# Moving the on-chip arenas of a hybrid encoder kernel to other addresses

## The chip, the cores and the metric

The kernel runs on one core of a Trainium2 chip. Its engines are TensorE (PE, with its weight loads shown apart as PEld), VectorE (DVE), ScalarE (ACT), GpSimd (POOL) and SyncE (SP), which here issues the DMAs. Operands live in the on-chip memory, 128 partitions wide; TensorE writes its products to eight banks of PSUM. The metric is the time of one execution on the device in microseconds; the kernel before has a median of 2407.32 us over two runs.

## The reference

One layer of a bidirectional encoder is applied to two sequences, a prompt of 512 tokens and a sample of 1024 tokens, of width 1024, all in float32:

```
h    = rms_norm(x, n_pre_mix)
proj = h @ w_in                                  # 1024 x 6688
y_a  = gated_delta(conv(q, k, v), g, beta) both ways, normed, gated @ w_br_gdn
y_b  = hgrn2(q, f, i) both ways, normed, gated @ w_br_hg
x    = x + rms_norm((gate0 * y_a + gate1 * y_b) @ w_out, n_post_mix)
h2   = rms_norm(x, n_pre_ffn)
ff   = (silu(h2 @ w_gate) * (h2 @ w_up)) @ w_down    # 1024 -> 2816 -> 1024
y    = x + rms_norm(ff, n_post_ffn)
```

The gated delta rule and HGRN2 are computed in chunks with small matrix products; the large dense products are those with `w_in`, the two branch weights, `w_out`, `w_gate`, `w_up` and `w_down`.

## The kernel before

**Split products.** A dense product in float32 is made from three products of a rounded type (float32r): each operand x is split into a rounded part `hi` and the rest `lo = x - hi`, and `mm3` adds `hi*hi`, `hi*lo` and `lo*hi` in one bank. The function `split` does this with one ACT copy and one DVE subtraction, which write the two parts into an arena of type float32r. The stationary operand of such a matmul is 128 x 128, the moving one 128 x 512, and every matmul loads its own weights. Where the tokens allow it, the products are arranged in the seven-product scheme of Strassen and Winograd (`seven`, `p2_both`, `down`). The small products of the chunked recurrences are plain float32.

**Stages.** Projections and the two recurrences of both sequences run interleaved until about 1184 us; then come the branch and output products, the gate and up products of the feed-forward part (`alone`, `seven`), and `down` at the end.

**Order.** The kernel writes its own order. `Tape` collects all operations with a cost for each, `schedule` places tiles in slots of pools and sorts the operations by a simulated clock, and `emit` issues them in that order. This is finished before any address is known: only then are the arenas opened and a slot turned into an address by `home`. All engine instructions are recorded at one line, L632, so that rows of the profile are told apart by arena.

**Arenas.** An arena is one on-chip tensor with the slots of a pool side by side. They stand in this order, each starting where the one before it ends:

- from the left: `sa` (constants and small vectors), `ba` (16 slots of 516 words, raw weights and intermediates), `ra` (128 columns of ones, split type), `ha` (4 slots of 4096 words, the split activations h and, later, a ring of split weights), `wa` (6 slots of 1024 words, split weights);
- from the right: `sm` (small tiles), `la` (36 slots of 516 words).

Later `la` and `sm` are closed and `xr` (20 slots of 1024 words, split operands of the feed-forward part) takes their place from the right; `wa` is closed and `xa` opens at its start; at the end `ha` is closed and `da` opens at its start. The constant `SKEW` adds words to `xr`. A slot of `ba`, `la`, `xa` or `da` is 516 words, that is 2064 bytes, so that each next slot starts 16 bytes further modulo 512. The slots and slices of the split arenas are all multiples of 512 bytes, so that within one of them every operand of a matmul starts at the same address modulo 512: 288 in all of them before the change.

In the rows of the profile a matmul is written bank<-moving,stationary; one name stands for both where both lie in the same arena.

Of the kernel before, what the change touches and what calls it, by code (L numbers as in the profile page):

```python
# [12 lines left out]
F32 = mybir.dt.float32  # L13
F32R = mybir.dt.float32r
# [26 lines left out]
HOLD = ((3, 2, 1, 2), (2, 2, 2, 2))  # L41
MSTEP = (24, 28)
PAIR = False
SKEW = 48
URGENT = 100
PO = False
NVEC = 88
# [700 lines left out]
def layer(ctx, tc, x_p, x_s, w_out, n_post_mix, n_post_ffn, w_down, vec, xt_p, xt_s, w_in, w_br, w_gate, w_up,  # L748
# [74 lines left out]
    hpool, wpool = Pool("h", 4, KD * TB), Pool("w", NW, 1024)  # L823
# [1630 lines left out]
    def arena(stack, name, cols, dtype, **kw):  # L2454
        return stack.enter_context(tc.tile_pool(name=name, bufs=1, **kw)).tile([P, cols], dtype, name=name + "_a")

    col = {}
    ends = [0, 0]
    for p in small.values():
        if p.kind == "SB":  # L2460
            b = p in brief
            col[p] = ends[b]
            ends[b] += p.count * p.width
    sa = arena(ctx, "sa", ends[0], F32)
    ba = arena(ctx, "ba", 16 * big.width, F32)
    hs, rs = ExitStack(), ExitStack()
    ra = arena(ctx, "ra", P, F32R)
    ha = arena(hs, "ha", 4 * hpool.width, F32R)
    w1 = ExitStack()
    wa = arena(w1, "wa", NW * 1024, F32R)  # L2470
    sm = arena(rs, "sm", ends[1], F32, side="right")
# [8 lines left out]
    def home(v):  # L2480
# [3 lines left out]
        if p is big or p is xpool:  # L2484
            s = [s for s in p.segs if s.low <= v.at][-1]
            if s.name not in opened:
                if s.name == "xr":
                    rs.close()
                else:
                    w1.close()  # L2490
                    if s.name == "da":
                        hs.close()
                opened[s.name] = arena(w1 if s.name == "xa" else ctx, s.name, s.count * p.width + (SKEW if p is xpool else 0),
                                       F32R if p is xpool else F32, side="right" if p is xpool else "left")
# [69 lines left out]
```

## Time and profile before

| | |
|---|---|
| two runs | 2408.84 and 2405.81 us, median 2407.32 us |
| profiled execution | span 2403.8 us from first to last instruction; no other time of it is listed |
| outside the span | 2407.32 - 2403.8 = 3.5 us, taken from the median |
| TensorE clock granted, mean | 0.999 |
| instructions | 37624, of which 14046 matmuls and as many weight loads |
| busy | PE 99%, PEld 83%, DVE 73%, ACT 52%, POOL 32% of the span |
| DMA | 338.62 MB, mean 141 GB/s |

The page gives for a group of instructions its busy time, the mean duration of one and the idle time before them. A matmul's recorded duration is longer than its place in the stream, since matmuls overlap; what one costs is the distance from its start to the next one's start. That distance is had from the timeline, which gives the start of a run of equal instructions and their number.

### The profile page before, as it was taken

The page shows a single profiled execution, that of the slowest core. Times are in us where ns is not written, and L with a number is a line of the kernel's source. Part 1 is how long each engine was busy: PE and PEld are TensorE (multiplying, and loading weights), DVE is VectorE, ACT ScalarE, POOL GpSimd, SP SyncE. Part 2 cuts the span into 40 slices and gives each one's busy share as a digit, 9 for nine tenths or more (in the row PEclk, how much of TensorE's full clock was granted, in tenths as well). Part 3 has the DMA queues.
Part 4 walks back from the last instruction along what each step waited for, and adds up shares of the span by engine and source line. Part 5 has one row for each costly group of instructions (what it writes and reads, how often), then busy time and mean ns, then how long its engine had stood idle before and what let it go on. Part 6 is the DMA issues. An engine that isn't in the chain of part 4 may idle for free.

```text
span 2403.8 us, 37624 instructions
## 1 busy us (share of the span) xinstructions
PE 2384.2 (99%) x14046; PEld 1991.2 (83%) x14046; DVE 1747.9 (73%) x2820; ACT 1256.1 (52%) x2096; POOL 766.7 (32%) x1021
## 2 busy tenths in 40 slices
PE   8999999999999999999999999999999999999998
PEld 6888888888888888888888888888888888888887
DVE  7878798958859667758767894665887878545566
ACT  6756867646647546647433464444353534433343
POOL 0544426051602513412120001213677675200221
PEclk9999999999999999999999999999999999999999
DMA  5124633411231230332875263543454554674453
GB/s 211 60 78 152 210 102 112 135 55 53 89 84 50 79 97 31 98 97 88 289 287 186 103 225 109 189 152 101 158 178 171 186 183 154 209 251 140 151 204 125
DMA packets 193334, 338.62 MB, mean 141 GB/s; under 512 B 53104, under 2 KB 92528, under 8 KB 193152
## 3 DMA queue, kind: packets, MB, share of 16 engines
q1 hardware_dynamic: 193152, 336.23, 41.8%
q8 instruction: 110, 1.80, 0.3%
q14 instruction: 72, 0.59, 0.1%
HBM read 255.50 MB, written 80.66 MB: 140 GB/s over the span
## 4 chain that ended last, share of the span: by engine, by line
PE 91%; DVE 6%; ACT 1%; issue 1%; DMA 1%; SPq 0%; POOL 0%; DVEq 0%; POOLq 0%
PE bank L632 91%; DVE la_a L632 3%; DVE ba_a L632 2%; DVE wa_a L632 1%; ACT la_a L632 1%; ACT ba_a L632 0%; DVE sm_a L632 0%; DMA la_a<-dram_cr_sc 0%; SPq L632 0%; ACT wa_a L632 0%; DMA ba_a<-lay_w_in 0%; DMA la_a<-dram_w_sc 0%; DMA dram_u_sc<-la_a 0%; DVE da_a L632 0%; ACT ha_a L632 0%
## 5 line engine op out<-in xcount | busy, mean ns | idle before, releaser
L632 PE MATMUL bank<-ha_a,wa_a 128*128 128x512 f32 x5496 | 1321.5, 395 | 1.1 <-DVE wa_a L632 0.9
L632 PEld LDWEIGHTS bank<-ha_a,wa_a 128*128 128x128 f32 x5496 | 1018.4, 188 | 207.5 <-issue 3.3
L632 PE MATMUL bank<-xr_a 128*128 128x512 f32 x1386 | 314.3, 389 | 0.0
L632 PEld LDWEIGHTS bank<-xr_a 128*128 128x128 f32 x1386 | 260.3, 188 | 53.8
L632 PE MATMUL bank<-xr_a,ha_a 128*128 128x512 f32 x1200 | 275.3, 389 | 0.0
L632 PEld LDWEIGHTS bank<-xr_a,ha_a 128*128 128x128 f32 x1200 | 225.4, 188 | 46.6
L632 POOL TENSOR_TENSOR ba_a<-ba_a 128x512 f32<-128x512 f32 (+1 forms) x129 | 168.8, 1314 | 216.5 <-DVE ba_a L632 85.6
L632 ACT ACTIVATE la_a<-la_a 128x512 f32<-128x512 f32 (+1 forms) x300 | 192.7, 658 | 62.9 <-DVE la_a L632 44.5
L632 DVE TENSOR_TENSOR wa_a<-la_a,wa_a 128x1024 fp32r<-128x1024 f32 (+1 forms) x136 | 161.3, 1198 | 58.2 <-PE bank L632 46.7
L632 ACT ACTIVATE wa_a<-la_a 128x1024 fp32r<-128x1024 f32 (+1 forms) x136 | 133.2, 992 | 102.3 <-PE bank L632 96.5
L632 POOL TENSOR_TENSOR la_a<-la_a 128x256 f32<-128x256 f32 (+2 forms) x50 | 60.1, 1210 | 352.7 <-DVE la_a L632 265.7
L632 DVE TENSOR_TENSOR wa_a<-ba_a,wa_a 128x1024 fp32r<-128x1024 f32 (+1 forms) x102 | 115.4, 1147 | 70.4 <-PE bank L632 51.0
L632 ACT ACTIVATE wa_a<-ba_a 128x1024 fp32r<-128x1024 f32 (+1 forms) x102 | 92.9, 928 | 105.5 <-PE bank L632 91.6
L632 ACT ACTIVATE ha_a<-ba_a 128x512 fp32r<-128x512 f32 (+1 forms) x124 | 79.3, 645 | 130.0 <-PE bank L632 110.4
L632 DVE TENSOR_TENSOR ha_a<-ba_a,ha_a 128x512 fp32r<-128x512 f32 (+1 forms) x124 | 129.6, 1053 | 17.7 <-ACT ha_a L632 17.2
L632 POOL TENSOR_TENSOR la_a<-la_a,sm_a 128x30 f32<-128x30 f32 (+43 forms) x248 | 133.2, 537 | 18.2
L632 POOL TENSOR_TENSOR sm_a<-la_a 128x60 f32<-128x60 f32 (+39 forms) x155 | 76.7, 495 | 166.9 <-DMA la_a<-dram_u_sc 156.2
L632 ACT ACTIVATE ba_a<-ba_a 128x512 f32<-128x512 f32 (+1 forms) x181 | 112.7, 633 | 18.9 <-DVE ba_a L632 16.7
L632 DVE TENSOR_TENSOR la_a<-la_a 128x512 f32<-128x512 f32 (+2 forms) x170 | 116.5, 700 | 8.4 <-ACT la_a L632 7.6
L632 PE MATMUL bank<-wa_a,ha_a 128*128 128x512 f32 x528 | 120.1, 390 | 0.0
L632 DVE TENSOR_TENSOR xr_a<-da_a,xr_a 128x1024 fp32r<-128x1024 f32 (+2 forms) x60 | 71.1, 1199 | 64.1 <-ACT xr_a L632 48.1
L632 PEld LDWEIGHTS bank<-wa_a,ha_a 128*128 128x128 f32 x528 | 99.1, 188 | 20.5
(192 smaller groups left out, 3358.1 us busy)
## 6 DMA issues: line engine op xcount, KB each, us to landing
la_a<-lay_w_in SPq DMA_DIRECT2D x79, 512.0 KB, 5.8
ba_a<-lay_w_gate SPq DMA_DIRECT2D x36, 512.0 KB, 4.2
ba_a<-lay_w_up SPq DMA_DIRECT2D x33, 512.0 KB, 3.7
dram_a_sc<-xa_a SPq DMA_DIRECT2D x56, 256.0 KB, 2.1
ba_a<-lay_w_in SPq DMA_DIRECT2D x27, 512.0 KB, 5.5
ba_a<-w_ffn_down SPq DMA_DIRECT2D x24, 512.0 KB, 4.5
da_a<-dram_a_sc SPq DMA_DIRECT2D x22, 512.0 KB, 6.0
ba_a<-dram_a_sc SPq DMA_DIRECT2D x20, 512.0 KB, 5.2
```

Of the source, the lines that this page charges most:

```text
L632: f(*[m(a) for a in o.args], **{k: m(a) for k, a in o.kw.items()})
```

## The change

Three constants and two widths change. `sa` becomes 56 words (224 bytes) longer, so that everything to its right on the left side moves by 224 bytes; `ha` becomes 32 words (128 bytes) longer, so that `wa` moves by another 128; `xr` gets 8 words (32 bytes) more at its end, so that its start, counted from the right, moves down by 32. The added words are never used.

```diff
-SKEW = 48
+SKEW = 56
+LEAD, GAP = 56, 32
...
-    sa = arena(ctx, "sa", ends[0], F32)
+    sa = arena(ctx, "sa", ends[0] + LEAD, F32)
     ba = arena(ctx, "ba", 16 * big.width, F32)
     hs, rs = ExitStack(), ExitStack()
     ra = arena(ctx, "ra", P, F32R)
-    ha = arena(hs, "ha", 4 * hpool.width, F32R)
+    ha = arena(hs, "ha", 4 * hpool.width + GAP, F32R)
```

Starts modulo 512 bytes, before and after:

| arena | before | after |
|---|---|---|
| sa, sm, la | 128, 320, 256 | the same |
| ba | 32 | 256 |
| ra, ha, and da later | 288 | 0 |
| wa, and xa later | 288 | 128 |
| xr | 288 | 256 |

No instruction, wait or DMA is added, removed or moved in the order.

## The prediction

> **What bounds the kernel now.** I read the page first (engines, chain of waits), then the list of what TensorE waited for, then the chain in order of time.
>
> ```profile
> span 2403.8 us, 37624 instructions
> ...
> PE 2384.2 (99%) x14046; PEld 1991.2 (83%) x14046; DVE 1747.9 (73%) x2820; ACT 1256.1 (52%) x2096; POOL 766.7 (32%) x1021
> ...
> PE 91%; DVE 6%; ACT 1%; issue 1%; DMA 1%; SPq 0%; POOL 0%; DVEq 0%; POOLq 0%
> ```
> ```profile
> PE bank L632 <- ACT ba_a L632: 7.1, 1, 7.1
> PE bank L632 <- DVE la_a L632: 1.9, 3, 0.9
> PE bank L632 <- DVE wa_a L632: 1.1, 2, 0.9
> ```
> ```profile
> 1183.59 1212.79 PE bank L632 x5398
> ```
>
> TensorE is busy 99% of the span. It waited 7.1 us once, at the start, and 1.9 and 1.1 us in the next two groups of waits; the rest are smaller. From 1183.59 us to 1183.59 + 1212.79 = 2396.4 us the chain is TensorE alone, without a break. So the time is the sum of the distances between matmul starts, and an address matters if it changes that distance; nothing else has a place to show.
>
> **What a matmul costs now.** The groups of matmuls, shapes kept apart, give the number of each pairing of arenas (moving, stationary):
>
> ```profile
> L632 PE MATMUL bank<-ha_a,wa_a 128*128 128x512 f32 x5496 | 1321.5, 395 | 1.1 <-DVE wa_a L632 0.9 <-ACT wa_a L632 0.2
> ...
> L632 PE MATMUL bank<-xr_a 128*128 128x512 f32 x1386 | 314.3, 389 | 0.0
> L632 PE MATMUL bank<-xr_a,ha_a 128*128 128x512 f32 x1200 | 275.3, 389 | 0.0
> ...
> L632 PE MATMUL bank<-wa_a,ha_a 128*128 128x512 f32 x528 | 120.1, 390 | 0.0
> L632 PE MATMUL bank<-ha_a 128*128 128x512 f32 x480 | 112.1, 389 | 0.0
> ...
> L632 PE MATMUL bank<-wa_a,ra_a 128*128 128x512 f32 x72 | 27.9, 410 | 0.8 <-ACT wa_a L632 0.4 <-DVE wa_a L632 0.3
> ...
> L632 PE MATMUL bank<-xr_a,wa_a 128*128 128x512 f32 x120 | 27.5, 390 | 0.0
> ```
>
> That is 9282 split matmuls. The timeline of TensorE gives their distance, from the start of one run of equal matmuls to the start of the next:
>
> ```profile
> 1416.64 43.68 PE L632 MATMUL bank<-ha_a,wa_a 128*128 128x512 f32 x192
> ```
> ```profile
> 1663.16 13.76 PE L632 MATMUL bank<-xr_a,wa_a 128*128 128x512 f32 x60
> 1676.76 5.60 PE L632 MATMUL bank<-ha_a,wa_a 128*128 128x512 f32 x24
> 1682.20 13.76 PE L632 MATMUL bank<-xr_a,wa_a 128*128 128x512 f32 x60
> ...
> 1701.24 13.76 PE L632 MATMUL bank<-xr_a,ha_a 128*128 128x512 f32 x60
> 1714.84 5.38 PE L632 MATMUL bank<-ha_a 128*128 128x512 f32 x23
> ```
> ```profile
> 2082.04 314.32 PE L632 MATMUL bank<-xr_a 128*128 128x512 f32 x1386
> ```
>
> 60 matmuls from 1663.16 to 1676.76 are 13.60 / 60 = 226.7 ns each; the 24 of the next run (1676.76 to 1682.20) 226.7; the 60 with `ha` as weights (1701.24 to 1714.84) 226.7; the 1386 of `down`, less the 0.39 us tail of the last, (314.32 - 0.39) / 1385 = 226.7; the 192 at 1416.64, less such a tail, (43.68 - 0.39) / 191 = 226.6. One figure for all pairings, although the arenas lie tens of kilobytes apart. 9282 x 226.7 ns = 2104 us of the 2403.8. But every one of these operands starts at 288 modulo 512, so the rows do not say how this figure depends on the start.
>
> One thing shows that the figure is not rigid. After the engine has done small matmuls, a burst of split ones starts slower:
>
> ```profile
> 345.61 1.55 PE L632 MATMUL bank<-ha_a,wa_a 128*128 128x512 f32 x6
> 347.00 0.40 PE L632 MATMUL bank<-wa_a,ra_a 128*128 128x512 f32 x1
> ```
>
> Six matmuls take 347.00 - 345.61 = 1.39 us, 231.7 ns each, with no wait between them and the same residues. So the stream has a restart pace of 231.7 and a settled pace of 226.7.
>
> **The change part by part.** *Instructions.* The order is fixed before the addresses are, so all 37624 instructions, their waits and their queues stay: cost nothing, with one answer.
>
> *`ba`, `xa`, `da` and the other engines.* Slots of these arenas are 16 bytes apart modulo 512, so a group over many slots already averages over many starts:
>
> ```profile
> L632 ACT ACTIVATE la_a<-la_a 128x512 f32<-128x512 f32 x279 | 170.6, 628 | 45.8 <-DVE la_a L632 30.8 <-POOL la_a L632 5.9 <-DMA la_a<-lay_w_in 4.8
> ...
> L632 ACT ACTIVATE ba_a<-ba_a 128x512 f32<-128x512 f32 x179 | 110.6, 628 | 18.9 <-DVE ba_a L632 16.7 <-POOL ba_a L632 0.5
> ```
>
> 628 ns in `la` (256 plus steps of 16) and 628 ns in `ba` (32 plus steps): the same to the nanosecond, so 0.2% is a wide bound. ACT is idle 48% and DVE 27% of the span, and that idleness is what hides a change of a few ns here; without it, 0.2% of DVE's 1747.9 us would be 3.5 us. I take 0, bounds -4 and +4 us.
>
> *DMAs.* The raw weights land in `la`, `ba` and `da`:
>
> ```profile
> la_a<-lay_w_in SPq DMA_DIRECT2D x79, 512.0 KB, 5.8
> ...
> ba_a<-lay_w_in SPq DMA_DIRECT2D x27, 512.0 KB, 5.5
> ```
>
> The same weights take 5.8 us into `la` and 5.5 us into `ba`, whose 16 slots run through all multiples of 16 modulo 256 before and after. Loads run ahead of the splits, and DMA is 1% of the chain, some 24 us; a tenth of that either way, 2 us, is the bound. I take 0.
>
> *Plain float32 matmuls.* Their operands in `la` and `ba` have all starts in steps of 16, in `sm` and `sa` others:
>
> ```profile
> L632 PE MATMUL bank<-sm_a,la_a 128*128 128x128 f32 x318 | 55.7, 280 | 0.3 <-DVE sm_a L632 0.2
> ...
> L632 PE MATMUL bank<-la_a 128*128 128x128 f32 x350 | 50.1, 276 | 0.7 <-DVE la_a L632 0.7
> ```
>
> 280 and 276 ns, 1.4% apart over quite different mixtures of starts and of distances between moving and stationary start. This is the nearest row to an answer: TensorE reads the same memory here, and its pace does not visibly follow the address. But such a matmul streams half as fast as a split one: the kernel's own cost function has 2 x k/2.4 + 5.5 ns for each of its two passes over k columns, and k/2.4 + 13.5 for a split matmul, and that larger remainder, 13.5 against 5.5, is what a start might touch.
>
> *Split matmuls.* The pairings (moving, stationary) become 0 and 128 (5496 of them), 128 and 0 (528 and 72), 256 and 0 (1200), 256 and 128 (120): 7416 with unlike starts. 1866 keep like starts, 256 (1386) and 0 (480). All starts become multiples of 64, while 288 is 4.5 x 64. The price of one can go down by 13.5 - 5.5 = 8.0 ns (the remainder of the float32 kind is left) and up by 5.0 ns (231.7 - 226.7, the restart pace kept for good); over 9282 matmuls this is -74 to +46 us. I take 0, since the float32 rows, the only ones with mixed starts, lie nearest.
>
> The page TensorE: Matmul & The Clock Gate of the Trainium skill (Part 2, step by step) has two independent read ports, one for the moving operand and one for weight loads, so that loading the next weights takes nothing from the running matmul. By that rule, unlike starts of the two would be worth nothing, which is the sum I take; no run here tests it at full rate. The same page (section on the 56 ns gap) measures 215.7 ns for 512 columns of a 2-byte type; by it the split matmuls would come to 9282 x 11.0 ns = 102 us less, an estimate of about 2305 us, and the trace disagrees with its 226.7.
>
> The sum: 2403.8 + 0 in span, and with the 3.5 us around it 2407 us.
>
> **The rivals.**
>
> *The remainder goes with the start (faster).* If the moving operand is fetched in pieces of 64 bytes, a row of 2048 bytes from 288 touches 33 of them and from 0, 128 or 256 only 32. By the cost function 512 columns are 213.3 ns, a piece 213.3 / 32 = 6.7 ns, and the settled distance 226.7 is 34 pieces. One fewer is 220.0 ns: -6.7 x 9282 = -62 us, 2345 us. In another form, weight loads and streams that begin at the same residue collide, and unlike starts take the 8.0 ns off the 7416: -59 us, 2348 us; with all 9282, 2333 us. For it: 226.7 is a whole number of pieces and leaves an unexplained remainder that float32 lacks. Against it: nothing in the trace shows the pieces, and the half-rate rows show no dependence.
>
> *The streams no longer settle (slower).* The pace falls from 231.7 to 226.7 some matmuls after a restart, so something between consecutive reads falls into step. If that needs equal starts of moving and stationary operand, the 7416 unlike ones stay at 231.7: +5.0 x 7416 = +37 us, 2444 us; if it needs the old start, all do: +46 us, 2454 us; one whole piece more on all, 233.3, gives +62 us, 2469 us. For it: like starts are what all settled streams have. Against it: like starts are also what the slow bursts have. It decides in `down` and the gate and up products, where nothing interrupts; +2% (48 us) needs 5.2 ns on every split matmul.
>
> *The padding does not act* (arenas rounded to some larger unit): no time changes; it shares the forecast's number and I give it no chance of its own.
>
> **How the numbers follow.** No change: 0.41, of which little is a shift within the few us of the other engines. Faster: 0.34, nearly all at 2333 to 2348, more than 2% (48 us) below; 0.01 of it is smaller. Slower: 0.25, of which 0.16 is above 2455 and 0.09 between 2407 and 2455. So faster by over 2%: 0.33; within 2%: 0.41 + 0.01 + 0.09 = 0.51; slower: 0.16. Two per cent is about what a measurement of this kernel can tell from no change. The range reaches from 2332, the lower end of the faster cases, to 2455, the end of the mild slower ones; it leaves out the 0.16 above and a few hundredths below. The likeliest case alone has 2401 to 2413, from its 4 + 2 us either way.
>
> **What would show each step right or wrong.** If the forecast holds, the last run of TensorE's timeline, `xr` with 1386 matmuls, again lasts 314.3 us, and the chain again ends in about 1213 us of TensorE alone. At 220.0 ns that run lasts 305.1 us; at 231.7, 321.3 us. If only unlike starts matter, the run of `xr` alone stays and those of `xr` with `ha` (13.60 us for 60) and `ha` with `wa` change. Where the ACT groups at 628 ns or the landing of the weights at 5.5 us move by more than a few per cent, my zero for the other engines is wrong. The forecast as a whole is wrong if any long run of split matmuls has another distance than 226.7 ns.

## The result, and the profile after

The changed kernel takes 2434.39 us (two runs, 2433.62 and 2435.15) against 2407.32 us: 27 us more, a ratio of 1.0116 with a 95% interval of 1.0086 to 1.0145. The forecast was 2407, no change. The time lies inside the forecast range, but the interval excludes 1: the kernel became slower, and the forecast did not have it. The granted TensorE clock is 0.999 before and after.

The page of the changed kernel gives the span, the busy time of each engine and the chain that ended last by engine. (The kernel has one line more, so all its instructions are now recorded at L633.)

```profile
span 2431.9 us, 37624 instructions
...
PE 2414.2 (99%) x14046; PEld 1992.7 (82%) x14046; DVE 1744.3 (72%) x2820; ACT 1257.9 (52%) x2096; POOL 764.1 (31%) x1021
...
PE 96%; DVE 3%; ACT 1%; issue 0%; DMA 0%; POOL 0%; DVEq 0%; SPq 0%; ACTq 0%; POOLq 0%
```

The same instructions in the same numbers. The span grew by 2431.9 - 2403.8 = 28.1 us, and TensorE's busy time by 2414.2 - 2384.2 = 30.0 us: more than the span. The other engines stand within 3.6 us of before. TensorE's idle time shrank from 19.6 to 17.7 us, which fits a slower TensorE that lets the others catch up. The list of what TensorE waited for, and the long piece of the chain in order of time (start, length, engine, tile, count), say the same:

```profile
PE bank L633 <- ACT ba_a L633: 7.1, 1, 7.1
PE bank L633 <- DVE la_a L633: 0.9, 1, 0.9
PE bank L633 <- DVE wa_a L633: 0.8, 1, 0.8
```
```profile
1028.09 1396.43 PE bank L633 x6670
```

The first wait is the same, the two after it are smaller, and the unbroken piece of TensorE alone now begins 155 us earlier. There is no new wait. The time is in the matmuls themselves, and the groups by shape say in which (moving, stationary; busy us, mean ns of one):

```profile
L633 PE MATMUL bank<-ha_a,wa_a 128*128 128x512 f32 x5496 | 1347.9, 399 | 1.1 <-DVE wa_a L633 0.8 <-ACT wa_a L633 0.2
L633 PE MATMUL bank<-xr_a 128*128 128x512 f32 x1386 | 314.3, 389 | 0.0
L633 PE MATMUL bank<-xr_a,ha_a 128*128 128x512 f32 x1200 | 275.3, 389 | 0.0
L633 PE MATMUL bank<-wa_a,ha_a 128*128 128x512 f32 x528 | 123.4, 395 | 0.0
L633 PE MATMUL bank<-ha_a 128*128 128x512 f32 x480 | 112.0, 389 | 0.0
...
L633 PE MATMUL bank<-xr_a,wa_a 128*128 128x512 f32 x120 | 28.2, 394 | 0.0
L633 PE MATMUL bank<-wa_a,ra_a 128*128 128x512 f32 x72 | 28.2, 414 | 0.5 <-ACT wa_a L633 0.3
```

Against before: `ha`/`wa` +26.4 us, `wa`/`ha` +3.3, `xr`/`wa` +0.7, `wa`/`ra` +0.3; `xr` alone 0, `xr`/`ha` 0, `ha` alone -0.1. The sum is 30.6 us, as much as TensorE's growth of 30.0. Sorted by the starts that the change gave them:

| moving, stationary | starts after | stationary - moving | growth, us |
|---|---|---|---|
| ha, wa | 0, 128 | 128 | 26.4 |
| wa, ha and wa, ra | 128, 0 | -128 | 3.6 |
| xr, wa | 256, 128 | -128 | 0.7 |
| xr, ha | 256, 0 | -256 | 0.0 |
| xr, xr and ha, ha | alike | 0 | -0.1 |

Pairs 128 bytes apart pay, pairs 256 bytes apart do not, although their starts are unlike too. The timeline of the gate and up products (start, length, tiles, number of matmuls) gives the price of one:

```profile
1690.33 14.10 PE L633 MATMUL bank<-xr_a,wa_a 128*128 128x512 f32 x60
1704.26 5.75 PE L633 MATMUL bank<-ha_a,wa_a 128*128 128x512 f32 x24
1709.85 14.10 PE L633 MATMUL bank<-xr_a,wa_a 128*128 128x512 f32 x60
...
1729.37 13.77 PE L633 MATMUL bank<-xr_a,ha_a 128*128 128x512 f32 x60
1742.98 5.60 PE L633 MATMUL bank<-ha_a 128*128 128x512 f32 x24
1748.42 13.76 PE L633 MATMUL bank<-xr_a,ha_a 128*128 128x512 f32 x60
...
2110.18 314.32 PE L633 MATMUL bank<-xr_a 128*128 128x512 f32 x1386
```

From start to start, 60 `xr`/`wa` take 1704.26 - 1690.33 = 13.93 us, 232.2 ns each, and 24 `ha`/`wa` take 5.59 us, 232.9 each; before, both were 226.7. The 60 `xr`/`ha` (13.61 us) and the 24 of `ha` alone (5.44 us) are still at 226.8 and 226.7, and the last run of `xr` alone still lasts 314.32 us to the hundredth.

Of the groups that I had named for the other engines and the DMAs, the ACT groups stand at 628 ns as before, and the landing of the weights went from 5.8 and 5.5 us to 5.6 and 5.2:

```profile
L633 ACT ACTIVATE la_a<-la_a 128x512 f32<-128x512 f32 x279 | 170.6, 628 | 44.3 <-DVE la_a L633 32.9 <-POOL la_a L633 7.2 <-PE bank L633 1.9
L633 ACT ACTIVATE ba_a<-ba_a 128x512 f32<-128x512 f32 x179 | 110.7, 628 | 18.1 <-DVE ba_a L633 15.9 <-POOL ba_a L633 0.3
```
```profile
la_a<-lay_w_in SPq DMA_DIRECT2D x79, 512.0 KB, 5.6
...
ba_a<-lay_w_in SPq DMA_DIRECT2D x27, 512.0 KB, 5.2
```

### The profile page after: what moved, and what is told of

It reads as the page before. It is cut to its first block, busy times and chain, and to the rows that moved or that the text cites. A ratio compares the mean times of both kernels' runs of the same rounds, so it can differ in the third digit from the quotient of the medians.

```text
span 2431.9 us, 37624 instructions
## 1 busy us (share of the span) xinstructions
PE 2414.2 (99%) x14046; PEld 1992.7 (82%) x14046; DVE 1744.3 (72%) x2820; ACT 1257.9 (52%) x2096; POOL 764.1 (31%) x1021
## 4 chain that ended last, share of the span: by engine, by line
PE 96%; DVE 3%; ACT 1%; issue 0%; DMA 0%; POOL 0%; DVEq 0%; SPq 0%; ACTq 0%; POOLq 0%
PE bank L633 96%; DVE la_a L633 2%; DVE ba_a L633 0%; DVE wa_a L633 0%; DMA la_a<-lay_w_in 0%; ACT ba_a L633 0%; ACT la_a L633 0%; DVE sm_a L633 0%; ACT wa_a L633 0%; DVE da_a L633 0%; POOL sm_a L633 0%; DVE sa_a L633 0%; ACT sm_a L633 0%; POOL la_a L633 0%; DVEq L2560 0%
## 5 line engine op out<-in xcount | busy, mean ns | idle before, releaser
L633 PE MATMUL bank<-ha_a,wa_a 128*128 128x512 f32 x5496 | 1347.9, 399 | 1.1 <-DVE wa_a L633 0.8
L633 PEld LDWEIGHTS bank<-ha_a,wa_a 128*128 128x128 f32 x5496 | 1020.6, 189 | 230.9 <-issue 3.2
L633 PE MATMUL bank<-xr_a 128*128 128x512 f32 x1386 | 314.3, 389 | 0.0
L633 PEld LDWEIGHTS bank<-xr_a 128*128 128x128 f32 x1386 | 260.1, 188 | 54.0
L633 PE MATMUL bank<-xr_a,ha_a 128*128 128x512 f32 x1200 | 275.3, 389 | 0.0
L633 PEld LDWEIGHTS bank<-xr_a,ha_a 128*128 128x128 f32 x1200 | 225.2, 188 | 46.8
L633 POOL TENSOR_TENSOR ba_a<-ba_a 128x512 f32<-128x512 f32 (+1 forms) x129 | 166.7, 1298 | 228.4 <-DVE ba_a L633 90.7
L633 ACT ACTIVATE la_a<-la_a 128x512 f32<-128x512 f32 (+1 forms) x300 | 192.6, 658 | 59.4 <-DVE la_a L633 46.1
L633 DVE TENSOR_TENSOR wa_a<-la_a,wa_a 128x1024 fp32r<-128x1024 f32 (+1 forms) x136 | 162.5, 1207 | 64.8 <-PE bank L633 52.8
L633 ACT ACTIVATE wa_a<-la_a 128x1024 fp32r<-128x1024 f32 (+1 forms) x136 | 133.3, 992 | 108.1 <-PE bank L633 102.5
L633 POOL TENSOR_TENSOR la_a<-la_a 128x256 f32<-128x256 f32 (+2 forms) x50 | 60.1, 1211 | 361.3 <-DVE la_a L633 266.5
L633 DVE TENSOR_TENSOR wa_a<-ba_a,wa_a 128x1024 fp32r<-128x1024 f32 (+1 forms) x102 | 114.8, 1141 | 74.1 <-PE bank L633 53.0
L633 ACT ACTIVATE wa_a<-ba_a 128x1024 fp32r<-128x1024 f32 (+1 forms) x102 | 92.9, 928 | 113.0 <-PE bank L633 94.9
L633 ACT ACTIVATE ha_a<-ba_a 128x512 fp32r<-128x512 f32 (+1 forms) x124 | 79.3, 645 | 130.3 <-PE bank L633 111.5
L633 DVE TENSOR_TENSOR ha_a<-ba_a,ha_a 128x512 fp32r<-128x512 f32 (+1 forms) x124 | 128.2, 1041 | 18.9 <-ACT ha_a L633 18.7
L633 POOL TENSOR_TENSOR la_a<-la_a,sm_a 128x30 f32<-128x30 f32 (+43 forms) x248 | 127.1, 513 | 18.2
L633 POOL TENSOR_TENSOR sm_a<-la_a 128x60 f32<-128x60 f32 (+39 forms) x155 | 80.3, 518 | 165.9 <-DMA la_a<-dram_u_sc 155.2
L633 PE MATMUL bank<-wa_a,ha_a 128*128 128x512 f32 x528 | 123.4, 395 | 0.0
L633 DVE TENSOR_TENSOR la_a<-la_a 128x512 f32<-128x512 f32 (+2 forms) x170 | 116.0, 698 | 9.4 <-ACT la_a L633 8.4
L633 ACT ACTIVATE ba_a<-ba_a 128x512 f32<-128x512 f32 (+1 forms) x181 | 112.8, 633 | 18.1 <-DVE ba_a L633 15.9
L633 PEld LDWEIGHTS bank<-wa_a,ha_a 128*128 128x128 f32 x528 | 99.2, 188 | 23.7
L633 DVE TENSOR_TENSOR xr_a<-da_a,xr_a 128x1024 fp32r<-128x1024 f32 (+2 forms) x60 | 71.1, 1199 | 64.1 <-ACT xr_a L633 42.8
```

What stands on the lines that cost most here:

```text
L633: f(*[m(a) for a in o.args], **{k: m(a) for k, a in o.kw.items()})
```

## The experiments

**Does the pace go with one start, with the other, or with the distance?** In the changed kernel the starts and the distances move together. A small kernel of matmuls alone pulls them apart: 16 moving operands of the split type, 128 x 512, and 16 stationary ones, 128 x 128, each next one starting 32 bytes later modulo 512; every pair gets a run of 44 equal matmuls. It computes nothing of the layer and was run once.

```python
for m in mov:
    for w in sta:
        ...
        for r in range(44):
            nc.tensor.matmul(ps, w[:, k * P:(k + 1) * P], m[:, 0:512], ...)
```

> A kernel that computes nothing of the layer: it holds 16 moving operands (128x512, split type), which start at 0, 32, ... 480 modulo 512 bytes, and 16 stationary ones with the same starts, and runs 44 matmuls of each of the 256 pairs one after the other. Theory D (the distance between the two starts decides): the distance in time of two matmuls is 226.7 ns on the diagonal and where the starts are 256 apart, and 232 to 233 ns where they are 128 apart, whatever the starts themselves; the other distances lie between 220 and 236 ns and repeat along the diagonals. Theory O (an operand's own start decides): whole rows or whole columns of the table are slow, that of the stationary start 128 among them, also where the moving start is 128. Theory S (settling): all pairs can settle at 226.7 and some only take longer; then the last matmuls of each run of 44 are at 226.7.

The timeline of this kernel, for the moving operand `me`, which starts at 128; the stationary ones `wa`, `wb`, ... start at 0, 32, ... (start, length, tiles, count):

```profile
665.86 10.43 PE L47 MATMUL bank<-me,wa 128*128 128x512 f32 x44
676.12 10.43 PE L47 MATMUL bank<-me,wb 128*128 128x512 f32 x44
686.39 10.24 PE L47 MATMUL bank<-me,wc 128*128 128x512 f32 x44
696.46 10.43 PE L47 MATMUL bank<-me,wd 128*128 128x512 f32 x44
706.73 10.14 PE L47 MATMUL bank<-me,we 128*128 128x512 f32 x44
716.71 10.42 PE L47 MATMUL bank<-me,wf 128*128 128x512 f32 x44
```

Start to start: `wa`, 128 below the moving start, 10.26 / 44 = 233.2 ns; `wc`, 64 below, 10.07 / 44 = 228.9; `we`, at the same start, 9.98 / 44 = 226.8; `wf`, 32 above, 233.2. Over all 256 pairs, with the mean of the last 24 of each run (worked out from the single starts), one number decides, the stationary start less the moving start, modulo 256:

| distance, bytes | 0 | 32 | 64 | 96 | 128 | 160 | 192 | 224 |
|---|---|---|---|---|---|---|---|---|
| ns | 226.7 | 233.3 | 233.3 | 234.2 | 232.8 | 233.3 | 228.9 | 233.3 |

Pairs of one distance agree within about 1 ns, wherever the two start, and a distance of 256 is as good as 0. So, for these starts in steps of 32 bytes, neither operand's own start nor its being a multiple of 64 counts, and each of the other seven distances costs more than 0. Of the theories in the expectation, D, the distance, holds; O and S do not.

**Which part of the change costs the 27 us?** The change moves `ba`, `xa`, `da` and `xr` as well. Three kernels take it apart. The ratios from here on are to the kernel before, run again beside them: median 2406.21 us over 19 runs here, 2406.68 us over 7 runs for the two kernels of the next question. The first keeps everything but the 128 bytes between `ha` and `wa`:

```diff
-LEAD, GAP = 56, 32
+LEAD, GAP = 56, 0
```

> The change without the 32 words after the split activations: h and the split weights start at 0, xr at 256, ba at 256. Theory D: all pairs are 0 or 256 apart, so every long run of split matmuls is at 226.7 ns and the time is that of the kernel before, 2407 us (within 4 us). Theory O: the weights no longer start at 128, 2407 us as well. If the moved raw-weight slots or the other engines cost the 27 us, it stays at 2434.

It took 2406.61 us, 1.0003 of the kernel before (0.9993 to 1.0013). Its groups:

```profile
L633 PE MATMUL bank<-ha_a,wa_a 128*128 128x512 f32 x5496 | 1322.1, 395 | 1.1 <-DVE wa_a L633 0.9 <-ACT wa_a L633 0.2
...
L633 PE MATMUL bank<-wa_a,ha_a 128*128 128x512 f32 x528 | 120.1, 389 | 0.0
```

1322.1 and 120.1, as before the change. So the lead ahead of `ba`, the new residues of `ba` and `da`, and the move of `xr` to 256 cost nothing together; nor does the move of `xa`, which starts at 0 here and at 128 in the change.

The second puts every split arena at 128, to see whether the own start counts where the distance is 0:

```diff
-SKEW = 56
-LEAD, GAP = 56, 32
+SKEW = 88
+LEAD, GAP = 88, 0
```

> All split operands start at 128 (88 words of lead, no gap, xr with 88 words more). Theory D: every pair is 0 apart, 2407 us. Theory O: every matmul now has operands at 128, which was the start in all slow pairs, so all 9282 are at 232 ns or more: 2407 + 9282 x 5.3 ns = 2456 us.

2406.31 us, 0.9999 (0.9990 to 1.0009). The start by itself has no price.

The third is the reverse: the old starts, with nothing added but the 128 bytes:

```diff
-SKEW = 56
-LEAD, GAP = 56, 32
+SKEW = 48
+LEAD, GAP = 0, 32
```

> The kernel before with only the 32 words after the split activations: h and xr stay at 288, the split weights go to 416, 128 further. Theory D: the pairs with the weights (5496 + 528 + 120) are 128 apart and slow again, about 2434 us. Theory O, with the start 128 as the cause: no operand starts at 128, 2407 us.

2435.04 us, 1.0119 (1.0104 to 1.0134), and the groups grow as with the whole change (1347.9 and 123.4 us there):

```profile
L633 PE MATMUL bank<-ha_a,wa_a 128*128 128x512 f32 x5496 | 1347.7, 399 | 1.0 <-DVE wa_a L633 0.8 <-ACT wa_a L633 0.2
...
L633 PE MATMUL bank<-wa_a,ha_a 128*128 128x512 f32 x528 | 123.3, 395 | 0.0
```

The one pad is the whole effect.

**Does the table predict a kernel that it has not seen?** Distance 192 has a small price (2.2 ns) one way round and 6.6 the other, since -192 is 64 modulo 256. And a distance between `xr` and the rest should slow other groups than the change did.

```diff
-SKEW = 56
-LEAD, GAP = 56, 32
+SKEW = 48
+LEAD, GAP = 0, 48
```

> The kernel before with the split weights 192 bytes further (h and xr 288, weights 480). By the table of starts, weights 192 beyond the moving operand cost 228.9 ns and weights 64 beyond (the same as 192 short of it) 233.3: +2.2 ns on 5496 + 120 matmuls and +6.7 ns on 528, +15.9 us for settled streams. In the change the table's +6.1 ns on 6144 matmuls would have been 37.5 us and 27 came, since the short bursts of the first half are off the pace anyway; by the same share +11.5 us. So 2418 to 2422 us. If only a distance of 128 were bad, 2407.

2421.34 us, 1.0061 (1.0044 to 1.0078), inside the expected 2418 to 2422. The groups show both directions (`ha` moving with `wa` at distance 192, `wa` moving with `ha` at 64):

```profile
L633 PE MATMUL bank<-ha_a,wa_a 128*128 128x512 f32 x5496 | 1333.1, 397 | 1.1 <-DVE wa_a L633 0.9 <-ACT wa_a L633 0.3
...
L633 PE MATMUL bank<-wa_a,ha_a 128*128 128x512 f32 x528 | 123.6, 395 | 0.0
```

1333.1 - 1321.5 = 11.6 us over 5496 is 2.1 ns each, and 123.6 - 120.1 = 3.5 us over 528 is 6.6 ns each, nearly the table's 2.2 and 6.7. The expectation had also scaled the 15.9 us of the table down to 11.5, as in the change; the time is 14.7 us above the 2406.68 run beside it, so that scaling was not borne out. The other kernel leaves `ha` and `wa` together and moves `xr` by 128:

```diff
-SKEW = 56
-LEAD, GAP = 56, 32
+SKEW = 16
+LEAD, GAP = 0, 0
```

> The kernel before with xr alone moved, to 416, 128 from h and the split weights. The pairs xr with h as weights (1200) and xr with the split weights (120) become 128 apart; xr with xr (1386) does not. By the table +6.1 ns on 1320 matmuls of long streams: +8.0 us, 2414 to 2415 us. If an operand's own start mattered, the 1386 would change as well: +16 us.

2417.29 us, 1.0043 (1.0028 to 1.0058), 10.6 us more than the 2406.68 of the kernel before beside it, 2.6 us above the expected 8.0 and beyond its 2414 to 2415.

```profile
L633 PE MATMUL bank<-xr_a 128*128 128x512 f32 x1386 | 314.3, 389 | 0.0
L633 PE MATMUL bank<-xr_a,ha_a 128*128 128x512 f32 x1200 | 283.1, 395 | 0.0
...
L633 PE MATMUL bank<-xr_a,wa_a 128*128 128x512 f32 x120 | 28.3, 395 | 0.0
```

The group that the change had left alone, `xr`/`ha`, is now the one that pays: 283.1 - 275.3 = 7.8 us, 6.5 ns each, and `xr`/`wa` 0.8 us. `xr` alone, which moved as a whole, stays at 314.3. The remaining 2 us are not in these groups. They lie ahead of the first matmul that reads `xr`, which starts at 1666.12 us instead of 1663.16: TensorE waits more often for DVE in the interleaved part (1.9 and 1.1 us before):

```profile
PE bank L633 <- DVE la_a L633: 3.3, 5, 0.9
PE bank L633 <- DVE wa_a L633: 2.0, 4, 0.9
```

Of the arenas only `xr` has moved, nothing touches it before 1498 us, and these waits have all ended by 1187 us. So this is no price of a distance; why the waits came out longer in this execution is not shown.

**Is there a better distance than 0, and does the float32 kind share the effect?** A second small kernel goes through 64 distances in steps of 4 bytes, then narrower weights (32 columns), shorter streams (256 columns), plain float32, and two alternations of pairs in which the weights being loaded and the running pair have different distances. It leaves the layer out too and was run once; the paces are means of the last 24 matmuls of a run.

> Again only streams of matmuls, nothing of the layer. (a) One moving operand at 0, stationary ones 0, 4, 8, ... 252 bytes further, 44 matmuls each. If the pairing in steps of 32 bytes is all there is, each group of eight has the pace of its 32-byte step; if a start inside a step matters, some distance may be under 226.7 ns, down to 220 or 216, and the kernel before can be beaten. (b) Stationary operands of 32 columns instead of 128, at 0, 32, ... 224: if the reads of the weights are what disturbs the stream, a quarter of them leaves at most a quarter of the spread (1.9 ns of 7.5) and the pace at distance 0 falls under 226.7, to 216 to 220; if not, 226.7 to 234.2 as with 128. (c) Moving operands of 256 columns: half the stream and the same weights; the same spread of 7.5 ns if the weights disturb, half of it if the stream disturbs itself. (d) Plain float32, 512 columns: 430 ns for each of the two passes at every distance, within 1 ns. (e) Moving starts 0 and 128 in turn, each with weights of its own start: a matmul's own pair is 0 apart and the weights that are loaded while it streams are 128 away. If the weights being loaded count, this is slow (232 to 233 ns); if a matmul's own pair counts, 226.7. (f) The same with the weights exchanged: own pair 128 apart, the weights being loaded at the stream's own start: 226.7 and 232 to 233 the other way round.

The pace does change inside a step of 32 bytes. Its timeline at the distances 140 (`wed`), 144 (`wee`) and 148 (`wef`):

```profile
365.37 10.42 PE L58 MATMUL bank<-ma,wed 128*128 128x512 f32 x44
375.63 10.14 PE L58 MATMUL bank<-ma,wee 128*128 128x512 f32 x44
385.61 10.43 PE L58 MATMUL bank<-ma,wef 128*128 128x512 f32 x44
395.88 10.33 PE L58 MATMUL bank<-ma,weg 128*128 128x512 f32 x44
```

Start to start that is 233.2, 226.8 and 233.4 ns. No distance is under 226.7 ns. Beside 0, seven steps are at the same 226.7 (120, 132, 144, 156, 204, 228, 252); all others lie at 228.3 to 236.7. So at this length and width padding cannot beat the kernel before; it can only reach it. The plain float32 groups, at distances 0 and 128 (two passes, so x32 for 16 matmuls):

```profile
L58 PE MATMUL bank<-mf,fa 128*128 128x512 f32 x32 | 13.9, 592 | 0.0
...
L58 PE MATMUL bank<-mf,fe 128*128 128x512 f32 x32 | 13.9, 593 | 0.0
```

13.9 us at each of the eight distances; from start to start 429.2 ns a pass at all of them. At 512 columns the float32 kind does not depend on the distance in these steps of 32 bytes.

Two things went against what I expected. With 32 columns of weights the paces are 231.7, 240.0, 231.7, 230.5, 230.2, 233.5, 231.7 and 233.3 at the eight distances: a quarter of the weights to load, and yet no smaller spread, and distance 0 itself is slower. So the price is not simply the amount of weights that is read beside the stream. And the alternations decided nothing: equal starts within the pair while the weights for the next lie 128 away gave 228.3 ns, the reverse 230.0, both between 226.7 and 232.8. With 256 columns the best distance was no longer 0 but 192, and the spread (113.3 to 120.0, 6.7 ns) is nearer the full 7.5 than the half: by part (c) that speaks for the weights as what disturbs, by part (b) the 32 columns speak against it.

**Is 0 the best distance by itself, or only for this length?** Theory B holds that equal starts are free of collisions whatever the shape; theory P that the read of the weights and that of the moving operand must fall into step in time, so that the best distance moves with the length of the stream. A third small kernel varies the columns of the stream and of the weights, and alternates one operand; the layer is left out, and it was run once.

> Streams of split matmuls alone, nothing of the layer: one moving operand at 0 of 512, 448, 384, 256 and 128 columns with weights of 128 columns at 0, 32, ... 224, then 512 columns with weights of 96 and of 64 columns. Theory B (equal starts are good as such): distance 0 is the fastest at every length and width. Theory P (what counts is in which step of the 256-byte period the next weights are read while the stream has reached its end): the best distance moves with the length, as it did to 192 for 256 columns in the run before (113.3 ns against 120.0 at 0), and with the width of the weights; a distance with a pace of a whole number of 6.67 ns steps exists at each length, and it is 0 only for 512 columns with 128. Last, two alternations at 512 columns: weights at 0 and 128 in turn for a moving operand at 0, and one weight tile at 0 for moving operands at 0 and 128 in turn. If each pair had its own price they would be the mean of 226.7 and 232.8, 229.7 ns, in steady alternation of the two; if the sequence counts, something else.

Pace in ns by distance, mean of the last 24 of each run (rows: columns of the stream x columns of the weights):

| | 0 | 32 | 64 | 96 | 128 | 160 | 192 | 224 |
|---|---|---|---|---|---|---|---|---|
| 512 x 128 | 226.7 | 233.3 | 233.3 | 234.2 | 232.8 | 233.3 | 228.9 | 233.3 |
| 448 x 128 | 202.7 | 204.5 | 202.2 | 200.0 | 204.4 | 205.3 | 200.0 | 206.7 |
| 384 x 128 | 173.3 | 173.3 | 174.8 | 173.3 | 176.1 | 176.7 | 173.3 | 176.7 |
| 256 x 128 | 120.0 | 118.3 | 117.8 | 117.4 | 118.7 | 120.0 | 113.3 | 116.7 |
| 128 x 128 | 111.7 | 111.7 | 111.7 | 111.7 | 111.7 | 111.7 | 111.7 | 111.7 |
| 512 x 96 | 230.0 | 228.9 | 228.3 | 233.3 | 231.7 | 231.1 | 233.3 | 233.3 |
| 512 x 64 | 230.0 | 231.7 | 231.1 | 231.3 | 229.4 | 231.4 | 228.3 | 230.8 |

Two of the runs of 256 columns, in its timeline: distance 0 (`wa`) and 192 (`wg`).

```profile
221.57 5.44 PE L54 MATMUL bank<-ma,wa 128*128 128x256 f32 x44
226.85 5.37 PE L54 MATMUL bank<-ma,wb 128*128 128x256 f32 x44
...
252.88 5.15 PE L54 MATMUL bank<-ma,wg 128*128 128x256 f32 x44
257.87 5.29 PE L54 MATMUL bank<-ma,wh 128*128 128x256 f32 x44
```

(226.85 - 221.57) / 44 = 120.0 ns at distance 0, (257.87 - 252.88) / 44 = 113.4 at 192: here equal starts are the worst of the eight, with 160. So theory B is wrong. Of theory P, the best distance does move with length and width, but not everywhere: at 384 columns 0 is still among the best, with 32, 96 and 192, and at 128 columns all are alike. P's other claims missed: a pace of a whole number of 6.67 ns steps does not exist at every length (111.7 at 128 columns is none), and distance 0 has one at 384 and at 256 columns too, at 256 as one of the two slowest (120.0, 18 steps). With weights of 128 columns the best pace of each length from 256 on is a whole multiple of 6.67 ns: 17, 26, 30 and 34 of them. Alternating weights at 0 and 128 on one moving operand gave 232.2 ns on average, alternating two moving operands on one set of weights 230.0, each in a repeating cycle (235, 231, 226, 228 in the second). If each pair had a price of its own, both would lie halfway, at 229.7. The second is near that, the first is not, so the order of the pairs counts as well as the pairs.

## Why the prediction was wrong, and where it was right

**The step that failed** is the price of the split matmuls: "I take 0, since the float32 rows, the only ones with mixed starts, lie nearest". That row was no bound on a split matmul of 512 columns, for two reasons. It is another kind of instruction, which streams at about half the rate (429.2 ns a pass against 226.7 at 512 columns) and at 512 columns shows no dependence on the distance. And its matmuls have 128 columns, a length at which split streams show none either (111.7 ns at all eight distances); the prediction had not noticed that difference. Besides, 280 and 276 ns are mean durations of one, not distances from start to start, so they did not give the pace. The difference in rate the prediction had seen ("that larger remainder, 13.5 against 5.5, is what a start might touch") and still let the half-rate row decide. Measured, a settled split matmul costs 232.8 - 226.7 = 6.1 ns more at 128 bytes distance; the bounds were -8.0 and +5.0, so the upper one was too low as well, though not by much: +46 us over all split matmuls would have been +57.

**The rule of two read ports**, in the Trainium skill, page TensorE: Matmul & The Clock Gate (Part 2, step by step), was read as "unlike starts of the two would be worth nothing". For the half-rate kind the runs agree with that reading (429.2 ns throughout). For split matmuls at 512 columns they do not: only the distance between the moving and the stationary start changes, and the pace goes from 226.7 to as much as 234.2 ns. Whether this arises at a port or elsewhere no run shows, so the rule itself may stand; what failed is the inference from it.

**The slower rival came nearest**: it had the direction, and it had the cause in the relation of the two starts: "something between consecutive reads falls into step. If that needs equal starts of moving and stationary operand, the 7416 unlike ones stay at 231.7: +5.0 x 7416 = +37 us". Three of its sizes were off. The starts count modulo 256, not 512, so the 1200 `xr`/`ha` matmuls, 256 apart, kept their pace: 6216 pay, not 7416. The price of a settled one is 6.1, not 5.0. And not every one is settled: 26.4 us over 5496 `ha`/`wa` matmuls is 4.8 ns. Sorted by length (all 290 bursts, that is unbroken runs, of this group, from the start of a burst to the start of the next instruction, before and after), bursts of over 30 went from 228.4 to 234.1 ns each, bursts of 13 to 30 from 230.9 to 236.0 and bursts of 7 to 12 from 243.3 to 245.8, while those of 6 went from 243.3 to 244.7 and those of 2 to 5 stayed at 261.7 and 261.0. A short burst among small matmuls had little to lose. So too many matmuls and too low a price nearly cancel (6216 x 6.1 = 38 us against the rival's 37), which is luck, and the short bursts make the rest of the way down to 30.6 us in the groups and 28.1 us in the span.

Its picture of settling is not borne out. In the small kernel the unlike pairs run at paces of their own by distance, 228.9 to 234.2, over the whole run of 44 and not at one restart pace; and that restart pace, 231.7, was read from one burst of six, where all thirty bursts of six average 243.3. "For it: like starts are what all settled streams have" was evidence in the trace that the prediction gave too small a chance; "like starts are also what the slow bursts have" speaks only against equal starts being sufficient, and the rival needed them to be necessary.

**The faster rivals are out.** Pieces of 64 bytes would have made every start at a multiple of 64 faster: all starts at 128 gave 0.9999. Collisions of equal starts would have made unlike ones faster: in this kernel they are slower. What is left of the first is only the unit: 6.67 ns, which it took for a piece, turns up in the best pace of each length from 256 columns on.

**What was right.** Instructions, other engines and DMAs at 0: `gap0` moves all of `ba`, `xa`, `da` and `xr` and stands at 1.0003, and the ACT groups stayed at 628 ns. The landing of the weights in `ba` moved by more than the few per cent that the text had named as a warning (5.5 to 5.2 us), but it is 5.3, 6.0 and 5.9 us in `gap48`, `gap32only` and `skew16`, where `ba` keeps its old start, so it varies that much by itself. That nothing but the distance of matmul starts could carry an effect held: the split groups grew by 30.6 us, TensorE by 30.0. One sign that the text named came half true: for unlike starts the run of `xr` alone was to stay and those of `xr` with `ha` and `ha` with `wa` to change; `xr` alone stayed and `ha` with `wa` changed, and `xr`/`ha` staying at 13.61 us for 60 was the first sign that the period is 256.

**Two smaller sizes** were off. The text held that a measurement can tell about two per cent from no change; 19 runs of the kernel before lie within 0.16% (2404.55 to 2408.28 us), and 1.2% is clear. And the 3.5 us around the span mixed a median with the span of one faster execution: after the change, and in every run that lists both, the span and the time of the same execution are about 1.7 us apart.

**What stays open**: where the period of 256 bytes comes from; why narrow weights at distance 0 are slower; why alternations do not all give the mean of their pairs; why a distance of 128 is slow and 132 is not; and why TensorE waited 2 us longer ahead of `xr` in the kernel with `xr` moved by 128.

## What to carry to other kernels

Where full-rate split matmuls of 512 columns bound a kernel, keep the starts of the moving and of the stationary operand equal modulo 256 bytes: here 128 bytes of unused padding cost 1.2%, and padding that left the distance at 0 or 256 cost nothing. At other lengths another distance can be better (192 at 256 columns, 96 or 192 at 448), and at 384 columns 0 is among the best; a run of matmuls alone, one per distance, finds it. And in predicting, a row of another rate, type or length isn't a bound on the instruction in question, however near it looks; a property that all fast cases share deserves a fair chance of being what makes them fast.

## What the runs showed of the hardware that was not expected

The pace of a split matmul stream depends on the distance of its two operands' starts modulo 256 bytes, from 226.7 to 234.2 ns at 512 columns in steps of 32 bytes, up to 236.7 in steps of 4, and not on either start alone. Plain float32 of 512 columns (429.2 ns a pass) and split streams of 128 columns (111.7 ns) show nothing of it. The best distance can change with the length of the stream and the width of the weights, and at 256 columns the difference is the largest in proportion, 113.3 against 120.0 ns, 5.9%.
